# Feed-forward second product by seven Strassen block products, with GpSimd adding the blocks of h

## Chip, core and metric

One core of a Trainium2 chip runs the whole program. The metric is device microseconds of one execution; lower is better.

## What is computed

One layer of a diffusion transformer: sequence mixers, then a feed-forward block on 1024 tokens of width 1024, hidden width 2816, all in float32. The change touches the feed-forward block and the layer norm that ends the kernel:

```python
def conv_ffn(h, w_up, conv_w, conv_b, w_down, grid_rows):
    a, g = jnp.split(h @ w_up, 2, axis=-1)                 # first product
    ...
    a = dwconv3x3(a.reshape(...), conv_w).reshape(bsz, t, f) + conv_b
    return (jax.nn.gelu(a, approximate=False) * g) @ w_down  # second product
...
x_new = layer_norm(ALPHA * x_new + mx[5] * ffn_x, ln2_g[l], ln2_b[l])
```

## The kernel before

Every large product is made in three TensorE passes of 128x512: each operand is split into a high part (a copy by ScalarE rounded to float32r) and a low part (the remainder, by VectorE or GpSimd), and `mm3` adds high by high, high by low and low by high in PSUM.

**First product, `ffn_up`.** It runs over 22 hidden tiles ("units", f = 0 to 21) of 128 columns, each for the a half and the g half. It is already done by Strassen's method: per unit seven block products in the order k = 1, 2, 6, 5, 7, 3, 4, each of 12 matmuls. `prepare` makes the weight blocks five products ahead: the sums of blocks and the low parts on GpSimd (`pool.tensor_tensor`, 11 of them in a unit), the high parts on ScalarE. `Unit.after(k)` hangs the other work behind the products: behind k = 3 the convolution of the unit (eight VectorE operations), behind k = 6 of the next unit its GELU (ScalarE), behind k = 5 of the next unit the product with the gate (`Unit.finish`, VectorE), which stores the tile h of 128x1024 to DRAM (`hd[f]`). The buffers of this stage come from one ring of 13 (`S`), in order of allocation. In this stage the order on every engine is the order of the code (`pinned`).

**Second product, `ffn_down`.** Two passes, g = 0 and 1, over the tokens in halves of 512. In each pass all 22 hidden tiles are multiplied into eight PSUM banks (four token tiles t by two column halves c): 22 x 4 x 2 x 3 = 528 matmuls, 1056 in both. `down_load` loads weights `in_w_down` (tile `r`) and h (tile `hr`) on SyncE's queue and splits them into `dwh`, `dwl` and `dh`; the scheduler orders this stage. `down_first` prepares the first three hidden tiles beside the last unit of `ffn_up`, and their 72 matmuls open the stage. The last 3 tiles of pass 0 and the last 7 of pass 1 are held back (`late`) and multiplied token tile by token tile, so that VectorE can finish one token tile (`gate` product, `residual`, statistics, `finish`: the layer norm `ln_g`, `ln_b`, and the store of `out`) while TensorE works on the next.

## Time and profile before

| | |
|---|---|
| three runs | 1334.07, 1337.91, 1340.23 us; median 1337.91 |
| profiled execution | 1334.04 us; span of its instructions 1332.1 us |
| TensorE matmul, VectorE, ScalarE, GpSimd busy | 1275.0 (96%), 963.9 (72%), 536.7 (40%), 307.0 us (23%) |
| granted TensorE clock, mean | 0.995 |
| 700 to 1060 us (first product): TensorE, VectorE, GpSimd | 354.79, 264.25, 269.82 of 360 us; DMA 105 GB/s |
| 1078 to 1206 us (second product, most of pass 0): TensorE, VectorE, GpSimd | 124.71, 66.51, 4.34 of 128 us; DMA 180 GB/s |
| 1206 to 1332 us (most of pass 1): TensorE, VectorE, GpSimd | 116.46, 79.22, 0.00 of 126 us; DMA 154 GB/s |

Times in the trace count from the start of the span. PE is TensorE, DVE VectorE, ACT ScalarE, POOL GpSimd, SPq SyncE's queue, which issues nearly all DMAs. An instruction's row gives its start, its length, its engine, output and inputs, and in brackets how long the engine was idle before it and what ended that. A PE row's length holds the pipeline; the pace of matmuls is read from the starts of consecutive rows. The record lacks a few matmuls.

### The profile page before, as it was taken

How to read it: one execution, taken by the hardware profiler on the slowest of the kernel's cores; microseconds unless marked ns; L12 is line 12 of the kernel's file. 1: busy time of each engine (PE TensorE's matmuls, PEld its weight loads, DVE VectorE, ACT ScalarE, POOL GpSimd, SP SyncE). 2: the span in 40 equal slices, each digit the busy share in tenths (PEclk: the TensorE clock that was granted, in tenths of full speed). 3: DMA queues.
4: the chain of work that ended last, by engine and by line, in shares of the span. 5: the costliest groups of instructions: out<-in, count | busy, mean ns of one | idle time of the engine just before them, and what ended most of it. 6: DMA issues, size and time to landing. Idle time of an engine off the chain costs nothing. (4 is left out here: it accounts for less than half of the span.)

```text
span 1332.1 us, 17666 instructions
## 1 busy us (share of the span) xinstructions
PE 1275.0 (96%) x6480; PEld 1069.2 (80%) x6480; DVE 963.9 (72%) x1744; ACT 536.7 (40%) x972; POOL 307.0 (23%) x249
## 2 busy tenths in 40 slices
PE   4999999999999999999988999999999999999997
PEld 3888888899888887777876888888888878888885
DVE  7868975686769679689787787776667754359447
ACT  4835444433342241444553444444444434324420
POOL 0000000000000000000026777787767730000000
PEclk9999999999999999999998999999999999999999
DMA  9763343114122155355382344222222319448522
GB/s 332 257 199 118 108 131 126 48 62 143 35 87 88 48 163 190 100 199 191 127 238 81 125 158 158 104 102 95 96 68 76 119 65 322 142 136 273 175 94 81
DMA packets 88103, 181.82 MB, mean 136 GB/s; under 512 B 8768, under 2 KB 29904, under 8 KB 88016
## 3 DMA queue, kind: packets, MB, share of 16 engines
q1 hardware_dynamic: 85424, 171.25, 38.5%
q0 software_dynamic: 2592, 9.44, 1.9%
q8 instruction: 51, 0.84, 0.3%
q14 instruction: 36, 0.29, 0.1%
HBM read 150.23 MB, written 30.43 MB: 136 GB/s over the span
## 5 line engine op out<-in xcount | busy, mean ns | idle before, releaser
L57 DVE SCALAR_TENSOR_TENSOR psA<-a,par,psA 128x945 f32<-128x945 f32 (+2 forms) x176 | 215.9, 1227 | 21.7 <-ACT psA L57 16.2
L57 PE MATMUL psA<-x,wf 128*128 128x512 f32 x708 | 173.6, 395 | 6.5 <-ACT h L57 3.4
L57 PE MATMUL psB<-xk,wf 128*128 128x512 f32 x672 | 176.8, 390 | 1.0 <-ACT s L57 1.0
L57 PEld LDWEIGHTS psA<-x,wf 128*128 128x128 f32 x708 | 134.6, 190 | 36.2 <-ACT psA L57 4.3
L57 PEld LDWEIGHTS psB<-xk,wf 128*128 128x128 f32 x672 | 126.2, 188 | 27.9 <-ACT s L57 1.4
L57 POOL TENSOR_TENSOR wf<-raw,wf 128x512 fp32r<-128x512 f32 x95 | 122.4, 1297 | 54.4 <-ACT wf L57 54.3
L57 PE MATMUL psA<-xh,wh 128*128 128x512 f32 x320 | 126.7, 396 | 2.0 <-ACT wh L57 1.2
L57 PE MATMUL psA<-xh,wl 128*128 128x512 f32 x320 | 126.1, 394 | 0.1
L57 PE MATMUL psA<-xl,wh 128*128 128x512 f32 x320 | 125.9, 393 | 0.0
L57 POOL DMA_DIRECT2D wd<-pk x16 | 8.7, 543 | 498.9 <-ACT pk L57 461.3
L57 DVE TENSOR_TENSOR dwl<-r,dwh 128x512 fp32r<-128x512 f32 x74 | 48.4, 689 | 81.0 <-ACT dwh L57 80.9
L57 PE MATMUL psB<-x,wf 128*128 128x512 f32 x384 | 104.7, 389 | 0.0
L57 PE MATMUL psB<-dwh,dh 128*128 128x512 f32 x296 | 97.2, 389 | 2.6 <-ACT dh L57 2.6
L57 PE MATMUL psA<-dwh,dh 128*128 128x512 f32 x296 | 97.3, 390 | 0.5 <-DVE fy L57 0.5
L57 PEld LDWEIGHTS psB<-x,wf 128*128 128x128 f32 x384 | 72.1, 188 | 15.4 <-issue 0.2
L57 ACT CAST dwh<-r 128x512 fp32r<-128x512 f32 x74 | 43.0, 620 | 102.8 <-PE psA L57 63.4
L57 ACT CAST wh<-r 128x512 fp32r<-128x512 f32 x76 | 44.5, 619 | 84.3 <-PE psA L57 55.9
L57 ACT CAST wf<-raw 128x512 fp32r<-128x512 f32 x95 | 58.7, 618 | 47.8 <-PE psA L57 27.4
L57 DVE TENSOR_TENSOR a<-psA,s 128x512 f32<-128x512 f32 x39 | 27.0, 691 | 61.9 <-PE psA L57 61.9
L57 PEld LDWEIGHTS psA<-xh,wh 128*128 128x128 f32 x320 | 60.2, 188 | 14.0 <-ACT wh L57 1.6
L57 PEld LDWEIGHTS psA<-xh,wl 128*128 128x128 f32 x320 | 60.2, 188 | 12.3 <-DVE wl L57 0.5
L57 PEld LDWEIGHTS psA<-xl,wh 128*128 128x128 f32 x320 | 60.2, 188 | 11.8 <-issue 0.2
(324 smaller groups left out, 2761.2 us busy)
## 6 DMA issues: line engine op xcount, KB each, us to landing
r<-in_w_down SPq DMA_DIRECT2D x82, 256.0 KB, 3.2
raw<-in_wup SPq DMA_DIRECT2D x38, 512.0 KB, 4.9
ada<-in_ada SPq DMA_DIRECT2D x32, 512.0 KB, 4.4
r<-in_win SPq DMA_DIRECT2D x56, 256.0 KB, 2.9
hr<-hd SPq DMA_DIRECT2D x41, 256.0 KB, 4.3
hd<-h SPq DMA_DIRECT2D x20, 512.0 KB, 3.0
adat<-in_ada SPq DMA_DIRECT2D x16, 512.0 KB, 6.5
wd<-pk POOLq DMA_DIRECT2D x16, 512.0 KB, 3.6
```

Of the source, the lines that this page charges most:

```text
L57: ins = f(*args, **kw)
```

## The change

The second product is done by seven block products too. Tokens, hidden tiles and output columns are halved: h in blocks of 512 tokens by 11 hidden tiles, weights in blocks of 11 hidden tiles by 512 columns. A step is one product k and one of its 11 hidden tiles f: 4 token tiles by 3 passes, 12 matmuls. There are 77 steps, i = 0 to 76, in the order k = 1, 2, 6, 5, 3, 7, 4; 924 matmuls. Products 1, 6, 7 and 4 add up in four banks X, products 2, then 5 and 3, in four banks Y.

- **Sums of h.** For units f < 11, `sums` subtracts the two token halves of h on GpSimd and stores the 128x512 result (`s3`). For f of 11 and more, `fetch` loads the tile of unit f - 11 back and GpSimd makes two more sums (`s12`), one behind product 1 and one behind product 2 of the next unit; they go to DRAM too. That makes 11 + 22 GpSimd operations. In `ffn_up` the order on TensorE, VectorE and ScalarE is unchanged.
- **Sums of weights.** They are made on VectorE in the second product (`sum_t`, `sum_t4`, `sum_t3`: 22 + 11 + 11 operations), in tiles `tk`, `tv`, `tr` that stay in SBUF; before product 3, 11 more subtractions are made on h.
- **Operands.** `load` issues a step's DMAs eight steps ahead, `high` splits five steps ahead on ScalarE, `low` four steps ahead on VectorE (GpSimd for steps 3 and 4); eight pairs of split tiles are in flight. Every piece is 128x512 (256 KB). Three steps are prepared by `down_first`, 36 matmuls in place of 72. The SyncE queue is in program order; its load into `tv` (made by `stores`), the first of step 8, waits for TensorE's last use of step 2 (`dwv`), whose memory it takes.
- **Ends.** The four quarters of the output come ready at different times: work on them is put into a list `todo`, from which one piece a step is taken on VectorE (two in the first five steps of product 7). Products 5 and 7 hold their last 3 steps back and product 4 its last 5, to be multiplied by token tiles in the order (2, 3), (0), (1). Rows of x (`fx`) come by GpSimd's queue, a half tile each, and the first 512 tokens are stored by it too.

On GpSimd in the first product, one unit of the second half. Before (`wf` is a low part, `raw` a weight block, `s` its sum):

```order
L57 TENSOR_TENSOR wf_8410<-raw_8216,wf_8410 128x512
L57 TENSOR_TENSOR wf_8437<-s_8435,wf_8437 128x512
L57 TENSOR_TENSOR raw_8217<-raw_8216,raw_8217 128x512
L57 TENSOR_TENSOR wf_8453<-s_8433,wf_8453 128x512
L57 TENSOR_TENSOR raw_8216<-raw_8216,s_8435 128x512
L57 TENSOR_TENSOR wf_8479<-raw_8217,wf_8479 128x512
L57 TENSOR_TENSOR wf_8495<-raw_8216,wf_8495 128x512
L57 TENSOR_TENSOR wf_8517<-raw_8217,wf_8517 128x512
```

After; `s_8596` is the new tile of sums, `h_8509` the tile loaded back:

```order
L57 TENSOR_TENSOR wf_8489<-raw_8285,wf_8489 128x512
L57 TENSOR_TENSOR wf_8518<-s_8516,wf_8518 128x512
L57 TENSOR_TENSOR raw_8286<-raw_8285,raw_8286 128x512
L57 TENSOR_TENSOR wf_8534<-s_8514,wf_8534 128x512
L57 TENSOR_TENSOR raw_8285<-raw_8285,s_8516 128x512
L57 TENSOR_TENSOR wf_8560<-raw_8286,wf_8560 128x512
L57 TENSOR_TENSOR s_8596<-h_8509,h_8487 128x512
L57 TENSOR_TENSOR wf_8576<-raw_8285,wf_8576 128x512
L57 TENSOR_TENSOR s_8596<-s_8596,h_8509 128x512
L57 TENSOR_TENSOR wf_8600<-raw_8286,wf_8600 128x512
```

Two operations more stand between the low parts, the first of them behind a load.

On VectorE, second product. Before, in pass 1, only splitting while TensorE multiplies:

```order
L57 TENSOR_TENSOR dwl_10623<-r_10625,dwh_10622 128x512
L57 TENSOR_TENSOR dwl_10623<-r_10629,dwh_10622 128x512
L57 TENSOR_TENSOR dh_10624<-hr_10633,dh_10624 128x512
L57 TENSOR_TENSOR dhw_10780<-hr_10789,dhw_10780 128x512
L57 TENSOR_TENSOR dwl_10662<-r_10664,dwh_10661 128x512
L57 TENSOR_TENSOR dwl_10662<-r_10668,dwh_10661 128x512
L57 TENSOR_TENSOR dh_10663<-hr_10672,dh_10663 128x512
```

After, from the first use of product 3's finished banks, in product 7 (`fl` is a step's low part, `fy` an output half tile, `fx` its row of x, `bnd` its statistics):

```order
L57 TENSOR_TENSOR fy_9632<-fy_9632,psB_9617 128x512
L57 TENSOR_TENSOR fy_9656<-fy_9656,psB_9618 128x512
L57 TENSOR_TENSOR fl_10671<-dr_10608,fh_10670 128x512
L57 TENSOR_TENSOR fl_10671<-tk_9317,fh_10670 128x512
L57 TENSOR_TENSOR fy_9681<-fy_9681,psA_9619 128x512
L57 TENSOR_TENSOR fy_9704<-fy_9704,psA_9619 128x512
L57 TENSOR_TENSOR fl_10693<-dr_10628,fh_10692 128x512
L57 TENSOR_TENSOR fl_10693<-tk_9317,fh_10692 128x512
L57 TENSOR_TENSOR fy_9632<-fy_9632,gate_9322 128x512
L57 SCALAR_TENSOR_TENSOR fy_9632<-fx_10732,fy_9632 128x512
L57 BN_STATS bnd_9633<-fy_9632 128x6
L57 TENSOR_TENSOR fy_9656<-fy_9656,gate_9322 128x512
```

Between two steps' low parts there now stands the finishing of the first 512 tokens' second halves.

On VectorE at the end. Before, the last token tile, from its second half's product with the gate:

```order
L57 TENSOR_TENSOR fy_11045<-psB_10153,gate_9962 128x512
L57 SCALAR_TENSOR_TENSOR fy_11045<-fx_11046,fy_11045 128x512
L57 BN_STATS bnst_11048<-fy_11045 128x6
L57 BN_AGGR mvt_11097<-bnst_11048 128x2
L57 TENSOR_SCALAR vet_11099<-mvt_11097 128x1
L57 SCALAR_TENSOR_TENSOR fy_11045<-fy_11045,mvt_11097,ln_g 128x512
L57 RECIPROCAL rst_11100<-nwt_11102 128x1
L57 SCALAR_TENSOR_TENSOR fy_11045<-fy_11045,mvt_11097,ln_g 128x512
L57 TENSOR_TENSOR nwt_11102<-vet_11099,rst_11100 128x1
L57 SCALAR_TENSOR_TENSOR nwt_11102<-nwt_11102,rst_11100 128x1
L57 SCALAR_TENSOR_TENSOR rst_11100<-nwt_11102,rst_11100 128x1
L57 SCALAR_TENSOR_TENSOR fy_11045<-fy_11045,rst_11100,ln_b 128x512 x2
```

After, the last four rows of token tile 7 and the start of token tile 4; token tile 5 follows in the same way:

```order
L57 SCALAR_TENSOR_TENSOR fy_10406<-fy_10406,finmv_11130,ln_g 128x512
L57 SCALAR_TENSOR_TENSOR fy_10406<-fy_10406,finrs_11132,ln_b 128x512
L57 SCALAR_TENSOR_TENSOR fy_10406<-fy_10406,finmv_11130,ln_g 128x512
L57 SCALAR_TENSOR_TENSOR fy_10406<-fy_10406,finrs_11132,ln_b 128x512
L57 TENSOR_TENSOR fy_10418<-psB_9314,gate_9322 128x512
L57 SCALAR_TENSOR_TENSOR fy_10418<-fx_11169,fy_10418 128x512
L57 BN_STATS bnd_10419<-fy_10418 128x6
L57 BN_AGGR finmv_11174<-bnd_10419 128x2
L57 TENSOR_SCALAR finve_11175<-finmv_11174 128x1
L57 RECIPROCAL finrs_11176<-finw_11177 128x1
L57 TENSOR_TENSOR finw_11177<-finve_11175,finrs_11176 128x1
L57 SCALAR_TENSOR_TENSOR finw_11177<-finw_11177,finrs_11176 128x1
```

The product with the gate of token tile 4, whose bank is the last but one, stands behind eight layer norm operations of tiles 6 and 7.

The diff, cut to its core:

```diff
@@ Unit.after (first product, after each product k) @@
+            if k in (1, 2) and b.made:
+                b.made.sums()[k - 1]()
...
-                    b.prev = None
+                    b.prev.fetch()
+                    b.made = b.prev
...
+                if f == FT - 1:
+                    for part in b.made.sums():
+                        part()
                 self.conv()
@@ Unit, new @@
+        def fetch(self):
+            if self.f >= FT // 2:
+                self.h1 = self.new((2, 512), nm="h1")
+                self.b.nc.sync.dma_start(self.h1.rearrange("p g t -> p (g t)"), self.b.hd[self.f - FT // 2])
+        def sums(self):
+            b, pool, f = self.b, self.b.nc.gpsimd, self.f
+            def one():
+                if f < FT // 2:
+                    s3 = b.S((2, 512), nm="s3")[:, 0]
+                    pool.tensor_tensor(out=s3, in0=self.h[:, 0], in1=self.h[:, 1], op=ALU.subtract)
+                    b.nc.sync.dma_start(b.s3[f], s3)
+                else:
+                    self.s12 = self.new((2, 512), nm="s12")
+                    pool.tensor_tensor(out=self.s12[:, 0], in0=self.h1[:, 1], in1=self.h[:, 1], op=ALU.add)
+            def two():
+                if f >= FT // 2:
+                    s = self.s12
+                    pool.tensor_tensor(out=s[:, 1], in0=s[:, 0], in1=self.h1[:, 0], op=ALU.subtract)
+                    (b.nc.sync if f < FT - 2 else b.nc.gpsimd).dma_start(b.s12[f - FT // 2], s)
+            return one, two
+    HF = FT // 2
@@ down_first (prepared beside the last unit) @@
+            nc.sync.dma_start(r[f][:, 0], self.h_part(0, 0, f))
+            nc.sync.dma_start(r[f][:, 1], self.w_part(0, 0, f))
...
@@ ffn_down, new (the old one, down_load, load_xnew and finish go) @@
+        order = (1, 2, 6, 5, 3, 7, 4)
+        plan = [(k, f) for k in order for f in range(HF)]
+        N, LD, LP = len(plan), 8, 4
+        first = {k: HF * i for i, k in enumerate(order)}
+        group = {5: 3, 7: 3, 4: 5}
+        X = [self.bank("B"), self.bank("B"), *(lambda p: (p[:, 0], p[:, 1]))(self.pair())]
+        kq = [self.kp.tile([P, 8, 512], F32, tag="kq", bufs=2, name=self.name("tk")) for _ in range(2)]
...
+        def load(i):
+            k, f = plan[i]
+            if k == 1 and f == 8:
+                stores()
+            if k == 1:
+                nc.sync.dma_start(t1[f], self.w_part(0, 0, f))
+                if i < 3:
+                    return
+            r = raws[i] = raw()
+            h = {1: (0, 0), 2: (0, 1), 3: (0, 1), 4: (1, 1)}.get(k)
+            src = self.h_part(*h, f) if h else self.s3[f][:, :] if k == 7 else self.s12[f][:, 1 if k == 6 else 0]
+            nc.sync.dma_start(r[:, 0], src)
+            w = {2: (1, 0), 3: (1, 1)}.get(k)
+            if w:
+                nc.sync.dma_start(r[:, 1], self.w_part(*w, f))
+            if k == 3:
+                exs[i] = self.Rt(nm="s2")
+                nc.sync.dma_start(exs[i], self.s12[f][:, 1])
+        def load_t(f):
+            e = ts[f] = extra()
+            for phi in range(2):
+                nc.sync.dma_start(e[:, phi], self.w_part(phi, 1, f))
+        def sum_t(f):
+            e = ts.pop(f)
+            tt(out=t1[f], in0=e[:, 0], in1=t1[f], op=ALU.subtract)
+            tt(out=t2[f], in0=e[:, 1], in1=t1[f], op=ALU.subtract)
...
+        def high(i):
+            k, f = plan[i]
+            if i % 8 < 3:
+                x = forms[i] = [self.Wt((2, 512), nm="dw") for _ in range(2)]
+            else:
+                x = forms[i] = [dn.tile([P, 2, 512], F32R, tag=t, bufs=5, name=self.name(t)) for t in ("fh", "fl")]
+            if k == 3:
+                tt(out=raws[i][:, 0], in0=raws[i][:, 0], in1=exs.pop(i), op=ALU.subtract)
+            if k in (2, 3):
+                nc.scalar.copy(x[0], raws[i])
+            else:
+                for j, src in enumerate(source(i)):
+                    nc.scalar.copy(x[0][:, j], src)
+        def low(i):
+            k, f = plan[i]
+            x = forms[i]
+            on = nc.gpsimd if i < 5 else nc.vector
+            if k in (2, 3):
+                on.tensor_tensor(out=x[1], in0=raws[i], in1=x[0].bitcast(F32), op=ALU.subtract)
+            else:
+                for j, src in enumerate(source(i)):
+                    on.tensor_tensor(out=x[1][:, j], in0=src, in1=x[0][:, j].bitcast(F32), op=ALU.subtract)
+            raws.pop(i)
+        def multiply(i, t):
...
+            b = (Y if k in (2, 5, 3) else X)[t]
+            mm(b, hi[:, 0, s], hi[:, 1], start=k in (1, 2, 5) and f == 0, stop=False, skip_group_check=True)
+            mm(b, lo[:, 0, s], hi[:, 1], start=False, stop=False, skip_group_check=True)
+            mm(b, hi[:, 0, s], lo[:, 1], start=False, stop=f == HF - 1, skip_group_check=True)
...
+        def out(t, c, bank, add):
+            x, y = {}, new_y(t)[:, half[c]]
+            def fetch():
+                x[0] = dn.tile([P, 512], F32, tag="fx", bufs=3, name=self.name("fx"))
+                nc.gpsimd.dma_start(x[0], self.xnew[t][:, half[c]])
+            def begin():
+                if add:
+                    tt(out=y, in0=y, in1=bank, op=ALU.add)
                 else:
+                    fetch()
+                    tt(out=y, in0=bank, in1=gate[:, half[c]], op=ALU.mult)
+            def mid():
+                fetch()
+                tt(out=y, in0=y, in1=gate[:, half[c]], op=ALU.mult)
+            def end():
+                self.residual(x[0], y, st[t][:, c, :])
+            if add:
+                return begin, mid, end
+            return begin, end
...
+        def chain(*ts):
+            n = len(ts)
+            mv, ve, rs, w = (x[:, 0:n] for x in smalls())
+            for j, t in enumerate(ts):
+                nc.vector.bn_aggr(out=mv[:, j, :], in_=st[t])
+                stat[t] = mv[:, j, 0:1], rs[:, j:j + 1]
+            nc.vector.tensor_scalar(out=ve, in0=mv[:, :, 1], scalar1=EPS, scalar2=None, op0=ALU.add)
+            self.rsqrt2(rs, ve, n, w)
+        def last(t, c):
+            m, r = stat[t]
+            y, s = ys[t][:, half[c]], half[c]
+            nc.vector.scalar_tensor_tensor(out=y, in0=y, scalar=m, in1=lng[:, s], op0=ALU.subtract, op1=ALU.mult)
+            nc.vector.scalar_tensor_tensor(out=y, in0=y, scalar=r, in1=lnb[:, s], op0=ALU.mult, op1=ALU.add)
+            (nc.gpsimd if t < 4 else nc.sync).dma_start(self.out[t * P:(t + 1) * P, s], y)
...
+        sums = [(load_t, sum_t, 6, 2), (load_t4, sum_t4, first[6] + 1, 1), (load_t, sum_t3, first[5] - 2, 2)]
+        for i in range(N):
+            k, f = plan[i]
+            if i + LD < N:
+                load(i + LD)
+            for l, _, at, by in sums:
+                j = i - at + 3
+                if j >= 0 and j % by == 0 and j // by < HF:
+                    l(j // by)
+            if i + LP + 1 < N:
+                high(i + LP + 1)
+            if i + LP < N:
+                low(i + LP)
+            if i == 0:
+                u = self.prev
+                u.new = lambda shape, nm: extra()
+                u.gelu()
+                u.fetch()
+                u.finish()
+                for part in u.sums():
+                    part()
+            for _, g, at, by in sums:
+                j = i - at
+                if j >= 0 and j % by == 0 and j // by < HF:
+                    g(j // by)
...
+            n = group.get(k, 0)
+            if f < HF - n:
                 for t in range(4):
+                    multiply(i, t)
+            elif f == HF - 1:
+                if k == 4:
+                    for g in todo:
+                        g()
+                    todo = []
+                for part in ((2, 3), (0,), (1,)):
+                    for t in part:
+                        for j in range(i - n + 1, i + 1):
+                            multiply(j, t)
+                    for t in part:
+                        if k == 5:
+                            nc.scalar.copy(new_y(4 + t)[:, half[1]], Y[t])
+                        elif k == 7:
+                            b, *e = out(4 + t, 1, X[t], True)
+                            b()
+                            todo += e
+                        else:
+                            for g in out(4 + t, 0, X[t], False):
+                                g()
+                    if k == 4:
+                        chain(*(4 + t for t in part))
+                        for t in part:
+                            for c in range(2):
+                                last(4 + t, c)
...
+            if f == 0 and k == 5:
+                for x in zip(mids, ends):
+                    todo += x
+            if f == 0 and k in (6, 7):
+                o = [out(t, 0 if k == 6 else 1, Y[t], True) for t in range(4)]
+                todo += [x[0] for x in o]
+                mids, ends = [x[1] for x in o], [x[2] for x in o]
+                if k == 7:
+                    fin = [lambda t=t, c=c: last(t, c) for t in range(4) for c in range(2)]
+                    todo += [mids[0], both(ends[0], mids[1]), both(ends[1], mids[2]), both(ends[2], mids[3]), both(ends[3]),
+                             both(lambda: chain(0, 1, 2, 3), fin[0]), *fin[1:]]
+            for _ in range(2 if k == 7 and f < 5 else 1):
+                if todo:
+                    todo.pop(0)()
```

More of the change, by code (lines that the diff above doesn't have):

```diff
@@ L243, in build @@
             self.hd = [self.dp.tile([P, T], F32, name=f"hd{f}") for f in range(FT)]
+            self.s12 = [self.dp.tile([P, 2, 512], F32, name=f"s12_{f}") for f in range(FT // 2)]
+            self.s3 = [self.dp.tile([P, 512], F32, name=f"s3_{f}") for f in range(FT // 2)]
             self.xr = [self.dp.tile([P, 2, 512], F32, name=f"xr{j}") for j in range(4)]
@@ L1218, in ffn_up @@
         go(u1, 7)
[L1219 removed]
+        tt(out=u1.r[1], in0=u1.x, in1=u1.r[0], op=ALU.add)
         self.prepare(self.at + 5)
@@ L1255, in ffn_up @@
         self.prepare(self.at + 5)
-        u1.finish((u1.x, u1.r[:, 1]))
+        u1.finish((u1.x, u1.r[1]))
         u2.conv()
-        self.prev = u2
+        u1.sums()[0]()
+        self.prev, self.made = u2, None
         for f in range(3, FT):
@@ new lines, in high, with low @@
+        def high(dst, f):
+            nc.scalar.copy(dst, r[f])
+        def low(dst, hi, f):
+            nc.gpsimd.tensor_tensor(out=dst, in0=r[f], in1=hi.bitcast(F32), op=ALU.subtract)
+        def ahead(k):
+            y = self.ready
+            if k in (2, 7):
+                f = (2, 7).index(k)
+                y[f] = [self.Wt((2, 512), nm="dwh")]
+                high(y[f][0], f)
+            elif k in (6, 3):
+                f = (6, 3).index(k)
+                y[f].append(self.Wt((2, 512), nm="dwl"))
+                low(y[f][1], y[f][0], f)
+            elif k == 5:
+                v = self.kp.tile([P, 4, 512], F32R, tag="vt", bufs=1, name=self.name("dwv"))
+                y[2] = [v[:, 0:2], v[:, 2:4]]
+                high(y[2][0], 2)
+                low(y[2][1], y[2][0], 2)
@@ L1447, in ffn_down @@
                     self.row(n, r)
-            gate, lng, lnb = rows
-            ys = []
-            for t in range(4):
-                y = dn.tile([P, D], F32, tag="fy", bufs=4, name=self.name("fy"))
-                if g == 1:
-                    x = self.load_xnew(dn, 4 + t)
-                    st = self.small([2, 6], nm="bnst")
-                for c in range(2):
-                    for l in late:
-                        work(t, c, *l)
-                    s = slice(c * 512, (c + 1) * 512)
-                    nc.vector.tensor_tensor(out=y[:, s], in0=banks[t][c], in1=gate[:, s], op=ALU.mult)
-                    if g == 1:
-                        self.residual(x, y, s, st[:, c, :])
-                if g == 1:
-                    self.finish(y, 4 + t, lng, lnb, st)
-                ys.append(y)
@@ L1495, in load_xnew @@
[L1495 to L1514 removed]
+                gate, lng, lnb = rows
@@ L1517, in layout, with residual @@
+        assert not todo
+    def residual(self, x, y, st):
+        nc = self.nc
+        nc.vector.scalar_tensor_tensor(out=y, in0=x, scalar=ALPHA, in1=y, op0=ALU.mult, op1=ALU.add)
+        nc.vector.bn_stats(out=st, in_=y)
 def layout(x):
```

221 lines of the change are left out of this document (92 added, 129 removed).

## Prediction

> **What bounds the kernel now.** I read the page first, then who waited for whom on TensorE in the second product, the start and end of that stage in order of time, VectorE's pace there, and last GpSimd and the DMA by stretches.
>
> ```profile
> core 0 of [0], span 1332.1 us
> PE 1275.0 (96%) x6480; PEld 1069.2 (80%) x6480; DVE 963.9 (72%) x1744; ACT 536.7 (40%) x972; POOL 307.0 (23%) x249
> PE psB L57 <- ACT dh L57: 2.6, 1, 2.6
> PE psB L57 <- POOL dwl L57: 0.7, 1, 0.7
> PE psA L57 <- DVE fy L57: 0.5, 1, 0.5
> 1075.45 2.88 PE L57 MATMUL psB<-xk,wf 128*128 128x512 f32 x12
> 1078.17 0.39 PE L57 MATMUL psB<-dwh,dhw 128*128 128x512 f32 x1
> 1304.85 18.15 PE psB L57 x80
> 1323.00 0.02 issue
> ```
>
> TensorE is the bound: 96% busy, and in the whole second product (from 1078) it waited three times, 3.8 us together. Twelve matmuls take 1078.17 - 1075.45 = 2.72 us, 0.2267 each. The second product opens at 1078.17, and by the chain of work that ended last its matmuls end at 1323.0: 244.8 us, of which 1056 x 0.2267 = 239.4 are pace, 3.8 waits and 1.6 unexplained. What follows 1323.0 is VectorE and a store:
>
> ```profile
> 1323.02 0.69 DVE L57 TENSOR_TENSOR fy<-psB,gate 128x512 f32<-128x512 f32 x1 [1.59 <-PE psB L57]
> 1323.75 0.69 DVE L57 SCALAR_TENSOR_TENSOR fy<-fx,fy 128x512 f32<-128x512 f32 x1
> 1324.48 0.69 DVE L57 BATCH_NORM_STATS2 bnst<-fy 128x6 f32<-128x512 f32 x1
> 1325.21 0.21 DVE L57 BATCH_NORM_AGGREGATE mvt<-bnst 128x2 f32<-128x12 f32 x1
> ...
> 1327.29 0.16 DVE L57 SCALAR_TENSOR_TENSOR rst<-nwt,rst 128x1 f32<-128x1 f32 x1
> 1327.48 1.41 DVE L57 SCALAR_TENSOR_TENSOR fy<-fy,rst,ln_b 128x512 f32<-128x512 f32 x2
> 1202.70 1.29 DVE L57 TENSOR_TENSOR dwl<-r,dwh 128x512 fp32r<-128x512 f32 x2
> 1203.91 0.69 DVE L57 TENSOR_TENSOR dh<-hr,dh 128x512 fp32r<-128x512 f32 x1
> 1204.52 1.29 DVE L57 TENSOR_TENSOR dwl<-r,dwh 128x512 fp32r<-128x512 f32 x2
> ```
>
> VectorE ends at 1327.48 + 1.41 = 1328.9 and the span at 1332.1 (first row above): the tail behind the last matmul is 9.1 us, 3.2 of it the store. VectorE's own pace is to be read here too: independent operations follow each other every 0.60 us (1202.70, two later 1203.91, the next 1204.52), dependent ones every 0.73 (1323.02, 1323.75, 1324.48, 1325.21).
>
> **The matmuls.** 1056 become 924: 132 x 0.2267 = -29.9 us, all on the path, since TensorE is the bound there. The three waits go with the code that made them: -3.8.
>
> **GpSimd in the first product.** One TensorE unit is 84 x 0.2267 = 19.04 us.
>
> ```profile
> L57 POOL TENSOR_TENSOR wf<-raw,wf 128x512 fp32r<-128x512 f32 x78 | 100.2, 1293 | 43.2 <-ACT wf L57 43.1
> L57 POOL TENSOR_TENSOR raw<-raw,raw 128x512 f32<-128x512 f32 x16 | 27.6, 1724 | 0.0
> 1000.00:1040.00 40.00, 40.00 (x178) 33.14 (x177) 27.23 (x28) 17.96 (x28) 29.86 (x25) 1.00 0.19 69
> 787.60 1.81 DVE L57 CUSTOM_DVE_ANT_0 ada<-ada,silc,par 128x1024 f32<-128x1024 f32 x1
> 788.30 2.27 POOL L57 TENSOR_TENSOR raw<-raw,raw 128x512 f32<-128x512 f32 x1
> 790.53 1.29 POOL L57 TENSOR_TENSOR wf<-s,wf 128x512 fp32r<-128x512 f32 x1
> 785.49 0.68 DVE L57 TENSOR_TENSOR h<-h,r 128x512 f32<-128x512 f32 x1
> raw<-in_wup SPq DMA_DIRECT2D x38, 512.0 KB, 4.9
> ```
>
> In the stretch from 1000 us GpSimd is busy 29.86 of 40 (the fifth pair of columns). A unit has 11 operations of 1.29: 14.2. Units from 11 on get two more, 16.8 of 19.04; the earlier ones one, 15.5. The low parts are begun four to five products before use, at least 10.9 us, so a low part that comes 2.6 later still comes in time: 0. What hides it is that lead; were it gone, the cost would be up to 2.6 x 11 = 29. The first sum waits for a tile of 512 KB loaded back, issued behind product 5, three products and more (8 us) ahead; loads of that size into `raw` land in 4.9. No wait is removed here, so no gain either.
>
> By the Trainium skill, "SBUF — State Buffer", section "Who interferes with whom", a VectorE operation with two SBUF inputs and a GpSimd operation that reads SBUF lock each other out. The rows agree: next to the 1.81 us operation on `ada` and `silc` GpSimd takes 2.27, else 1.29. By that rule units from 12 on, where VectorE has only the 0.68 us product `h<-h,r` of this kind, would lose up to about a microsecond each, 17.8 of 19.04, and the sum would be the same.
>
> **The start of the stage.** 36 matmuls are ready in place of 72, 8.2 us of cover for what step 3 needs.
>
> ```profile
> 1077.26 10.06 DVE L57 SCALAR_TENSOR_TENSOR psA<-a,par,psA 128x945 f32<-128x945 f32 x8 [0.85 <-ACT psA L57]
> 1078.15 2.37 POOL L57 TENSOR_TENSOR dwl<-dr,dwh 128x1024 fp32r<-128x1024 f32 x1
> 1057.82 36.60 SPq L57 DMA_DIRECT2D r<-in_w_down  x3
> 1094.47 0.42 SPq L57 DMA_DIRECT2D hr<-hd  x1
> r<-in_w_down SPq DMA_DIRECT2D x80, 256.0 KB, 3.2
> L57 ACT CAST dwh<-r 128x512 fp32r<-128x512 f32 x74 | 43.0, 620 | 102.8 <-PE psA L57 63.4 <-PE psB L57 20.3 <-DMA r<-in_w_down 14.4
> 1110.00:1114.00 4.00, 4.00 (x19) 3.31 (x18) 1.90 (x3) 1.72 (x3) 0.00 (x0) 1.00 1.03 355
> 1211.00:1217.00 6.00, 6.00 (x28) 4.96 (x27) 5.86 (x13) 3.33 (x6) 0.00 (x0) 1.00 0.86 249
> 1217.00:1223.00 6.00, 6.00 (x28) 4.98 (x27) 6.00 (x16) 1.87 (x4) 0.00 (x0) 1.00 0.96 307
> ```
>
> Before, SyncE's queue stood from 1057.82 to 1094 and TensorE still lost only 2.6. Now it can start when product 7 of the last unit frees `tk`, 5.4 us ahead of the stage. Up to step 3 it carries three pieces, three rows of 512 KB and two pieces, 2.9 MB: 8.2 us at 355 GB/s, and about 2 to land, so +5 in the stage. Two casts of 0.6 and two GpSimd operations of 1.29 make +8.8, against 8.2. Bounds: 0, and 5 (the old waits of 2.6 and 0.7 and half as much again); I take +1.5, nearest to the arithmetic. The queue's wait for `tv` holds all loads from step 8 on until step 2 is multiplied, +8.2; step 8 is needed at +21.8, so 0. VectorE's convolution ends at +9.2, and step 5, its first, is due at +13.6: 0.
>
> **DMA.** `load` and the sums of weights fetch 34, 26, 25 and 45 pieces in steps 3-13, 14-24, 25-35 and 36-46: 130 x 0.262 MB, with four pieces of x 35.1 MB in 44 x 2.72 = 119.7 us, 293 GB/s. The last stretches above carry 355, 249 and 307 GB/s at a DMA share of 1.03, 0.86 and 0.96, so 290 to 345 when full. The top stretch (11.8 MB in 29.9 us) falls behind by some 6 us, and pieces are issued eight steps, 21.8 us, ahead. Hidden: 0. Its ends: nothing at 293 and more, +10 at 270 (35.1 MB / 0.27 = 130 us).
>
> **VectorE up to product 7.**
>
> ```profile
> L57 DVE TENSOR_TENSOR kq<-kq,F 128x1024 f32<-128x1024 f32 x56 | 67.5, 1216 | 0.2
> ```
>
> Steps 0 to 54: convolution and gates 11.3, 64 low parts x 0.60, 22 of double width x 1.22, 44 sums of weights and 11 of h x 0.60, four adds, four finishing triples x 2.0: 120 us in 55 x 2.72 = 149.6. It keeps up: 0.
>
> **VectorE from product 7 to the end.** The order lists 138 operations from the first use of the finished Y banks:
> - 34 low parts x 0.60 = 20.4
> - 8 adds from a bank x 0.60 = 4.8
> - 12 triples (gate, residual, statistics), 0.73 + 0.73 + 0.60, some interleaved: 12 x 2.0 = 24.0
> - 16 half tiles of layer norm, two operations, 1.41 by the row of 1327.48: 22.6
> - 4 chains of small operations. 1325.21 to 1327.48 is 2.27 with two operations of 0.66 inside; bounds 0.95 and 2.27, I take 1.7, since ScalarE's root lies within: 6.8
>
> That is 78.6, and 1 for x behind the stores on GpSimd's queue: 79.6. TensorE's 22 steps are 59.8. So here VectorE is the bound: it ends 79.6 after the begin of product 7, plus 3.2 for the store, 82.8, where TensorE and the old tail would give 59.8 + 9.1 = 68.9. Cost +13.9. When TensorE waits for a bank that VectorE hasn't read yet, that is within this chain and isn't counted again. Bounds: 110 wide operations at 0.60 and 28 small ones at 0.16 are 70.5, +4.8; all wide ones at 0.73 are 91.6, about +26.
>
> **Sum.** -29.9 - 3.8 + 1.5 + 13.9 = -18.3: the profiled execution's 1334.04 becomes 1315.7. That execution is the fastest of before, 3.9 under the median of 1337.91, which would give 1319.6; I take 1317 for a median.
>
> **Rivals.**
> - DMA is the bound in steps 3 to 46. For it: 293 GB/s asked, and one full stretch that did 290. Against: 345 and 320 in the others. At 270 it gives 1317 + 10 = 1327; to cancel all gain it would have to fall to 250. The Trainium skill, "DMA: Bandwidth & Descriptors", section "Measured", says to batch to 1 MiB for 75% of peak; pieces of 256 KB would fall short of 290 by its table. The stretches were made of such pieces and reached 307 and 355, so the trace speaks against it.
> - All finishing stays hidden as far as VectorE's bound allows (70.5 us): 1317 - 9 = 1308. For it: operations of different tiles alternate. Against: inside a triple and a half tile each waits for the one before.
> - GpSimd becomes the bound in units 11 to 21, and the kernel slower. At 1.72 an operation (the row above, beside a VectorE operation of two SBUF inputs) 13 are 22.4, 3.3 over a unit: 11 units lose 36, less some 8 of lead: 1317 + 28 = 1345. It decides from 1.65 us an operation. Against: at 1000 us, with conv and gates running, GpSimd took 1.29.
>
> **How the numbers follow.** VectorE's end chain 0.60, DMA bound 0.22, finishing hidden 0.10, GpSimd bound 0.05, anything else 0.03. Half a per cent, 6.7 us, is what a measurement of this kernel can tell from nothing: faster is below 1331.2. The first and third case are all below it, the second mostly (0.15 of 0.22): 0.85 faster, 0.09 the same, 0.06 slower. The range reaches from the case of hidden finishing, 1307, over that of the DMA to 1330.
>
> **What would show it.** Of the profile after: PE 2.72 a step with a wait of 1 to 2 us at step 3; GpSimd 16.8 us a unit and no wait of PE for `wf`; VectorE without a pause from product 7 on and its work some 16 us past the last matmul, waits of PE for `psB` or `psA` on VectorE at the begin of product 4; the DMA share near 0.9 with no wait of PE for `fh`, `fl` or `dw` before product 7. Wrong would be: waits for low parts behind a DMA in steps 36 to 54, or for `wf` in the first product, or a tail below 12 us.

## The result, and the profile after

The changed kernel takes 1320.66 us in the median of four runs (1317.66, 1318.38, 1322.94, 1323.20), before 1335.99: a ratio of 0.9882 with a 95% interval of 0.9842 to 0.9922. The forecast was 1317.0 for a median and 1315.7 on the scale of the profiled execution, which took 1317.66. One of the nine runs of the kernel "low parts by GpSimd" in the table below took 3580.91 us; it is in that kernel's median and in none of the ratios.

The page of after, its waits of TensorE in the second product, the first matmul of that stage, and VectorE's rows at its end:

```profile
span 1315.9 us, 17639 instructions
PE 1244.5 (95%) x6348; PEld 1044.4 (79%) x6348; DVE 1016.8 (77%) x1790; ACT 550.5 (42%) x980; POOL 363.7 (28%) x309
PE psB L57 <- DVE fy L57: 2.9, 1, 2.9
PE psB L57 <- ACT fh L57: 1.5, 1, 1.5
PE psB L57 <- POOL fl L57: 1.1, 2, 0.7
PE psB L57 <- POOL dwl L57: 0.6, 1, 0.6
1076.23 0.39 PE L57 MATMUL psB<-dwh 128*128 128x512 f32 x1
1294.80 0.39 PE L57 MATMUL psA<-fl,fh 128*128 128x512 f32 x1
1230.21 1.37 DVE L57 TENSOR_TENSOR fy<-fy,psB 128x512 f32<-128x512 f32 x2 [4.13 <-PE psB L57]
1274.48 0.69 DVE L57 SCALAR_TENSOR_TENSOR fy<-fx,fy 128x512 f32<-128x512 f32 x1 [1.93 <-DMA fx<-xnew]
1288.42 0.69 DVE L57 TENSOR_TENSOR fy<-psA,gate 128x512 f32<-128x512 f32 x1 [1.81 <-PE psA L57]
1311.94 0.75 DVE L57 SCALAR_TENSOR_TENSOR fy<-fy,finrs,ln_b 128x512 f32<-128x512 f32 x1
```

From the first matmul of the second product to the end of the span ("the stage" below) it is 1315.9 - 1076.23 = 239.7 us, where it was 1332.1 - 1078.17 = 253.9: 14.3 less. The other 1.9 lie before the stage, whose start scatters from 1075.3 to 1079.9 in the runs below that leave the first product alone (once 1084.1); they aren't the change's. TensorE now ends 20.7 us ahead of the span, before 9.1, and VectorE works from 1230.21 to 1312.7 with 3.7 us of waiting inside: 1.93 for a row of x and 1.81 for token tile 2 from TensorE.

The stretches of GpSimd in the first product, and of the DMA in steps 3 to 46 (columns as before: GpSimd's busy time is the fifth pair; then granted clock, DMA share, GB/s):

```profile
980.00:1020.00 40.00, 40.00 (x178) 33.13 (x177) 27.93 (x28) 17.81 (x29) 34.72 (x28) 1.00 0.41 149
1085.00:1117.00 32.00, 29.40 (x120) 23.42 (x119) 21.13 (x26) 15.73 (x23) 11.15 (x11) 0.95 0.96 346
1117.00:1146.00 29.00, 29.00 (x129) 24.02 (x128) 26.72 (x38) 17.36 (x28) 0.00 (x0) 1.00 0.85 307
1146.00:1176.00 30.00, 30.00 (x134) 24.82 (x133) 27.07 (x45) 15.16 (x29) 0.55 (x1) 1.00 0.87 296
1176.00:1206.00 30.00, 30.00 (x133) 24.48 (x132) 23.78 (x35) 10.82 (x14) 1.64 (x3) 1.00 1.03 375
```

GpSimd is busy 34.72 of 40, 16.5 a unit, and TensorE 40.00 of 40. The DMA engines are busy for 0.85 to 1.03 of the time from 1085 to 1206, and no wait of TensorE for a load stands in the list above between step 3 and product 4.

The start of the stage, in rows of SyncE's queue, ScalarE and TensorE, and three stretches of 1 us:

```profile
1074.99 0.43 SPq L57 DMA_DIRECT2D dr<-hd  x1
1085.75 0.62 ACT L57 CAST fh<-dr 128x512 fp32r<-128x512 f32 x1 [10.46 <-DMA dr<-hd]
1086.94 0.50 PE L57 MATMUL psB<-fh 128*128 128x512 f32 x1 [1.54 <-ACT fh L57]
1089.01 0.50 PE L57 MATMUL psB<-fl,fh 128*128 128x512 f32 x1 [0.73 <-POOL fl L57]
1085.00:1086.00 1.00, 0.40 (x2) 0.00 (x0) 0.39 (x1) 0.25 (x1) 0.00 (x0) 1.00 1.06 406
1090.00:1091.00 1.00, 1.00 (x4) 0.76 (x3) 0.50 (x1) 1.00 (x3) 1.00 (x2) 0.50 1.06 408
1093.00:1094.00 1.00, 1.00 (x6) 0.83 (x5) 1.00 (x3) 0.60 (x2) 0.30 (x2) 1.00 1.02 375
```

h of step 3 was issued at 1074.99 and used at 1085.75, 10.7 us later, in which the DMA moved 358 GB/s. Behind the waits the granted clock was 0.50 until 1093: four matmuls a microsecond there. That loss stands in no wait; it is in "rest" in the table below.

### The profile page after: what moved, and what is told of

The parts are those of the page before. It is cut to its first block, busy times and chain, and to the rows that moved or that the text cites. A ratio compares the mean times of both kernels' runs of the same rounds, so it can differ in the third digit from the quotient of the medians.

```text
span 1315.9 us, 17639 instructions
## 1 busy us (share of the span) xinstructions
PE 1244.5 (95%) x6348; PEld 1044.4 (79%) x6348; DVE 1016.8 (77%) x1790; ACT 550.5 (42%) x980; POOL 363.7 (28%) x309
## 5 line engine op out<-in xcount | busy, mean ns | idle before, releaser
L57 POOL TENSOR_TENSOR wf<-raw,wf 128x512 fp32r<-128x512 f32 x95 | 123.2, 1301 | 19.9 <-ACT wf L57 19.3
L57 PEld LDWEIGHTS psA<-xh,wh 128*128 128x128 f32 x320 | 60.2, 188 | 14.3 <-ACT wh L57 1.6
L57 ACT CAST fh<-dr 128x512 fp32r<-128x512 f32 (+1 forms) x47 | 36.1, 768 | 82.1 <-PE psA L57 18.6
L57 PEld LDWEIGHTS psA<-xl,wh 128*128 128x128 f32 x320 | 60.2, 188 | 11.7 <-issue 0.2
L57 DVE TENSOR_TENSOR wl<-r,wh 128x512 fp32r<-128x512 f32 x76 | 50.1, 687 | 23.2 <-PE psB L57 13.2
L57 DVE TENSOR_TENSOR kq<-kq,F 128x1024 f32<-128x1024 f32 x56 | 67.6, 1217 | 0.2
L57 PE MATMUL psB<-kq,A 128*128 128x128 f32 x448 | 60.3, 288 | 0.8 <-ACT A L57 0.7
```

What stands on the lines that cost most here:

```text
L57: ins = f(*args, **kw)
```

## The experiments

All kernels in one table. Each ratio is to runs of before that were taken along with that kernel, so ratios are compared, not medians; stage, waits, rest and tail are those of one profile each. "Waits" are TensorE's in the stage; "rest" is what is left of the time to TensorE's end when these and 924 x 0.2267 = 209.5 us are taken off (before: 239.4); "tail" is from TensorE's end to the span's.

| kernel | median | ratio to before (95%) | stage | waits | rest | tail |
|---|---|---|---|---|---|---|
| before | | | 253.9 | 3.8 | 1.6 | 9.1 |
| after | 1320.66 | 0.9882 (0.9842 to 0.9922) | 239.7 | 6.1 | 3.4 | 20.7 |
| after, second time | 1318.32 | 0.9893 (0.9866 to 0.9919) | 242.6 | 6.3 | 6.0 | 20.8 |
| rows loaded late | 1317.59 | 0.9868 (0.9844 to 0.9892) | 236.5 | 3.6 | 2.7 | 20.7 |
| low parts by GpSimd | 1326.23 | 0.9937 (0.9911 to 0.9963) | 248.1 | 10.6 | 7.3 | 20.7 |
| eight steps held | 1322.40 | 0.9906 (0.9880 to 0.9932) | 239.6 | 9.7 | 8.7 | 11.7 |
| both of these | 1327.66 | 0.9945 (0.9925 to 0.9965) | 247.0 | 16.1 | 9.8 | 11.7 |
| sums three times | 1349.64 | 1.0115 (1.0091 to 1.0140) | 249.0 | 14.7 | 4.1 | 20.7 |
| low parts left out | 1313.37 | 0.9853 (0.9827 to 0.9878) | 235.1 | 2.9 | 1.9 | 20.7 |
| left out, eight held | 1315.97 | 0.9865 (0.9843 to 0.9887) | 235.9 | 7.9 | 6.9 | 11.7 |
| early finishing | 1310.44 | 0.9830 (0.9808 to 0.9851) | 232.0 | 2.0 | 1.2 | 19.3 |
| early, seven held | 1309.60 | 0.9821 (0.9800 to 0.9841) | 231.5 | 2.6 | 2.8 | 16.6 |
| more DMA (rows late) | 1332.28 | 0.9988 (0.9974 to 1.0001) | 254.9 | 14.1 | 10.6 | 20.7 |
| GpSimd, wait filled | 1323.97 | 0.9924 (0.9901 to 0.9947) | 245.0 | 3.9 | 4.0 | 20.7 |

**The control.** The changed kernel once more:

> The changed kernel once more, unaltered, as the measure for the others on the same chip: ratio to before 0.988, the stage (first matmul of the second product to the end of the span) 239 to 241 us, if its one profile is typical; a difference of more than 1.5 us would mean that differences of that size between the other profiles say nothing.

Measured: 242.6, so differences of up to 3 us between single profiles can be chance; what follows goes by waits and rows, and by stage only where more than that lies between. Where the 2.9 us are can be read, since 2.6 of them lie in "rest": at the start the clock stays halved for about 3 us longer, and TensorE's wait at product 4 is as long as in the first profile, but here the clock halves behind it. TensorE's row there, and three stretches of the second profile:

```profile
1268.42 0.77 PE L57 MATMUL psB<-dw 128*128 128x512 f32 x1 [2.85 <-DVE fy L57]
1094.13:1098.13 4.00, 4.00 (x13) 3.15 (x12) 4.00 (x6) 2.54 (x6) 2.70 (x3) 0.62 0.98 354
1266.00:1268.00 2.00, 0.00 (x0) 0.00 (x0) 2.00 (x4) 2.00 (x5) 0.11 (x1) 0.97 0.57 173
1268.00:1270.00 2.00, 1.58 (x4) 1.32 (x5) 1.97 (x4) 0.56 (x2) 0.00 (x0) 0.50 0.23 89
```

The times of the ten runs of this kernel go with their mean clock: 1315.33 to 1318.38 at 0.990 and 0.991, 1319.46 to 1323.20 at 0.988 to 0.986, 1326.88 at 0.984.

**The start: rows loaded late.**

```diff
-            if i == 2:
-                rows = [...]          # gate5, ln2_g, ln2_b: three loads of 512 KB
+            if i == 22:
+                rows = [...]
```

> Only the loads of the rows gate, ln_g and ln_b (three of 512 KB) are moved, from between step 2 and step 3 on SyncE's queue to step 22. After the change the second product takes 239.7 us from its first matmul (1076.23) to the end of the span (1315.9); its 36 ready matmuls run out and TensorE loses 2.6 us in three waits at step 3, and its next matmuls come at 0.32 to 0.43 us each for some 4 us. Theory 1, the DMA queue: h of step 3 is issued at 1075.0 and lands 10.7 us later, behind 1.5 MB of rows; at 390 GB/s these are 3.9 us. Without them the piece lands near 1082, the waits go, and since everything behind hangs on TensorE, the stage is 3 to 5 us shorter: 235 to 237. Theory 2, all loads in flight share the rate and the pieces of later steps move up: h of step 3 lands at most 1 us earlier and the stage stays within 1 us of 239.7. Theory 3, the stall goes but the rows collide with the loads of steps 20 to 30: a new wait of TensorE for fh or fl in steps 22 to 35, stage 237 to 240.

Measured: 236.5, where the first theory has it. The row that takes h of step 3, and the waits that are left:

```profile
1079.36 0.62 ACT L57 CAST fh<-dr 128x512 fp32r<-128x512 f32 x1 [2.98 <-DMA dr<-hd]
PE psB L57 <- DVE fy L57: 2.8, 1, 2.8
PE psB L57 <- POOL dwl L57: 0.6, 1, 0.6
PE psB L57 <- ACT fy L57: 0.2, 1, 0.2
```

The stage starts at 1077.32 here, so h of step 3 is there 2.0 us into it, in place of 9.5. The second theory, 1 us at most, is refuted by this; it is also more than the 3.9 us by which the rows alone would have held it up, because loads issued behind it share the rate: up to 1085.75 the changed kernel had moved 4.8 MB (323 GB/s from 1070.98 on), of which only 3.4 were issued ahead of that load or with it. The waits at step 3 are gone, 2.6 us, and with them the half clock behind them; no other took their place, except 0.2 at a bank. But "rest" falls by 0.7 only, since here the clock halves behind the wait at product 4. The gain of 3.2 us in the stage is no more than the scatter, and the ratios don't separate the two kernels; it is the row and the waits that show the effect. The tail is the same to 0.02: what TensorE gains at the start, the end keeps.

**The end, first pair.** GpSimd makes part of the low parts; product 4 holds eight steps; both.

```diff
                 for j, src in enumerate(source(i)):
+                    if k in (7, 4) and j:
+                        on = nc.gpsimd
...
-        group = {5: 3, 7: 3, 4: 5}
+        group = {5: 3, 7: 3, 4: 8}
-                for part in ((2, 3), (0,), (1,)):
+                for part in ((2,), (3,), (0,), (1,)) if k == 4 else ((2, 3), (0,), (1,)):
```

> The low parts of the weights in products 7 and 4 (22 operations, one of the two a step) are made by GpSimd in place of VectorE. From the begin of product 7 on VectorE has 17 operations of 0.60 fewer, 10.2 us. Theory A, the sum of VectorE's work sets the end (as the prediction had it): the stage, 239.7 us from the first matmul to the end of the span, becomes 230 to 232. Theory B, the order of the end sets it: from the last matmul on token tiles 2 and 3 (VectorE's wait for TensorE ends at 1288.4) VectorE has 24.3 us of finishing that can't begin earlier. Then only TensorE's wait of 2.85 us for VectorE at product 4 goes, and the stage becomes 236.9 (236.3 to 237.5), with the work behind the last matmul as long as before. Theory C, VectorE and GpSimd lock each other out: GpSimd's operations take 1.7 us or more in place of 1.29, VectorE's neighbours get longer too, and less than 2 us is gained or something lost.

> Product 4 holds back its last 8 steps in place of 5, and multiplies them one token tile at a time in the order 2, 3, 0, 1, so that VectorE may begin to finish token tile 2 earlier: 3 steps of 2.72 and 8 x 0.68 = 5.4 us behind the begin of product 4, near 1278.6, in place of 1288.4. Theory A (VectorE's sum of work sets the end): VectorE has the same work, the stage stays at 239.7 within 1.5. Theory B (the order of the end alone sets it): four token tiles of 6.4 us from 1278.6 end at 1304.2, 8.5 us earlier, stage 231. Theory A and B in series: VectorE is busy with low parts and the triples of product 7's quarter until 1286.6 whatever TensorE does, so four tiles of 6.4 end at 1312.2: the stage stays at 239 to 241.

> Both: GpSimd makes the low parts of the weights in products 7 and 4, and product 4 holds back 8 steps, one token tile at a time. Theory A (VectorE's sum): as with GpSimd's low parts alone, stage 230 to 232. Theory B (order alone): -11.4, 228, and the holding alone would give 231. Both in series: the one alone gives 2.9 us, the other alone none, and together they give more than the sum of the two, 6 to 11 us, stage 229 to 234; TensorE may lose a few us waiting for low parts of the last held steps, which it now needs earlier.

Measured: 248.1, 239.6, 247.0. GpSimd's help cost some 5 to 8 us: the third theory, but with the loss on VectorE's side. VectorE's groups from 1229 on in after (two rows), from 1236 on with GpSimd's help (two), and one pair of neighbours there:

```profile
L57 DVE SCALAR_TENSOR_TENSOR fy<-fy,finmv,ln_g 128x512 f32<-128x512 f32 x16 | 11.9, 746 | 0.0
L57 DVE TENSOR_TENSOR fy<-fy,gate 128x512 f32<-128x512 f32 x8 | 5.4, 680 | 0.0
L57 DVE SCALAR_TENSOR_TENSOR fy<-fy,finmv,ln_g 128x512 f32<-128x512 f32 x16 | 20.8, 1298 | 0.0
L57 DVE TENSOR_TENSOR fy<-fy,gate 128x512 f32<-128x512 f32 x8 | 11.9, 1482 | 0.0
1251.94 2.23 DVE L57 SCALAR_TENSOR_TENSOR fy<-fy,finmv,ln_g 128x512 f32<-128x512 f32 x1
1252.31 1.30 POOL L57 TENSOR_TENSOR dw<-tv,dw 128x512 fp32r<-128x512 f32 x1
```

These 24 VectorE operations took 8.9 + 6.5 = 15.4 us longer, more than the 10.2 that were taken off, so VectorE read its last X bank still later and TensorE's wait at product 4 grew from 2.9 to 6.9. Nothing else made VectorE late: ahead of the finishing behind token tile 2 it waited 1.4 us for TensorE, and for no row of x. An operation of two SBUF inputs that meets one of GpSimd's takes 2.23 in place of 0.75, while GpSimd's takes 1.30; of GpSimd's low parts behind the begin of product 7 only two took longer, 1.60 and 1.73. The Trainium skill, "SBUF — State Buffer", section "Who interferes with whom", has this as an exclusive lock between the two; these rows agree, and here it is VectorE that pays, though its row begins 0.37 us earlier. Because of this the pair doesn't decide between the theories; that eight held steps alone gain nothing (239.6) says only that VectorE isn't free earlier.

**The end, second pair.** The same relief without GpSimd:

```diff
+                    if k in (7, 4) and j:
+                        nc.scalar.copy(x[1][:, j], src)
+                        continue
```

> The low parts of the weights in products 7 and 4 are left out: ScalarE, which has time there, copies the block itself into their place, so the output differs. VectorE is relieved of the same 17 operations of 0.60 behind the begin of product 7 as when GpSimd made them, but without GpSimd beside it, which had made VectorE's operations longer (248.1 us for the stage). Theory A, the sum of VectorE's work alone sets the end: stage 239.7 - 10.2 = 229 to 231. Theory A and B in series: only TensorE's wait of 2.9 us at product 4 goes, since behind the last matmul of token tiles 2 and 3 the same 24.3 us of finishing follow: 236 to 237.5. If the stage stays near 248, it wasn't GpSimd that made the earlier kernel slow.

> The same low parts left out, and product 4 holds back 8 steps, one token tile at a time, which alone gained nothing (239.6). Theory A: as without the holding, 229 to 231. Both in series: relief and earlier token tiles together give more than the 2.9 of the one and the 0 of the other, 4 to 9 us: 231 to 236.

Measured: 235.1 and 235.9. With 10.2 us off VectorE the stage loses 4.6. Of these 0.3 are shorter waits at the start and 1.5 the clock (rest 1.9 in place of 3.4); the 2.8 that are left are TensorE's wait at product 4, as the theory in series has it. The sum of VectorE's work alone, 229 to 231, is refuted: 5.6 of the 10.2 us are missing, more than the scatter. TensorE's waits in the first of these, where none at product 4 is left, and VectorE's row where token tile 2 comes; then three rows of the second:

```profile
PE psB L57 <- ACT fh L57: 1.2, 1, 1.2
PE psB L57 <- POOL fl L57: 1.1, 2, 0.7
PE psB L57 <- POOL dwl L57: 0.6, 1, 0.6
1283.11 0.69 DVE L57 TENSOR_TENSOR fy<-psA,gate 128x512 f32<-128x512 f32 x1 [4.64 <-PE psA L57]
...
1263.71 0.69 DVE L57 TENSOR_TENSOR fy<-fy,psB 128x512 f32<-128x512 f32 x1 [1.35 <-PE psB L57]
1272.83 0.69 DVE L57 SCALAR_TENSOR_TENSOR fy<-fx,fy 128x512 f32<-128x512 f32 x1 [3.13 <-DMA fx<-xnew]
1291.38 0.69 DVE L57 TENSOR_TENSOR fy<-psA,gate 128x512 f32<-128x512 f32 x1 [2.43 <-PE psA L57]
```

Of the relief, 7.1 us turned into idling: VectorE waits 10.8 us behind its first use of the Y banks in place of 3.7, 4.64 of them ahead of token tile 2 (1.81 before), and behind that the same 24 us of finishing follow. With eight held the tail is short, 11.7, but VectorE's queue stands elsewhere, for TensorE (1.35, 2.43) and for a row of x (3.13), and TensorE's waits are 7.9. The two bounds in series are shown. That loosening both gives more than the sum is not: 235.9 lies inside the 231 to 236 expected, but relief alone gave 235.1, so the holding added nothing.

**GpSimd in the first product.** Each sum three times in units 11 to 21 (`for _ in range(3)` ahead of the two operations of `s12`).

> In units 11 to 21 GpSimd makes each sum of h three times (the same result written again): 17 operations of 1.29 us a unit, 21.9 us, in place of 13 (16.8), where TensorE's unit is 19.04. The prediction's reason why the sums cost nothing is that GpSimd has 2.2 us a unit left and the low parts are begun 11 us or more ahead. If so, the cover is now gone: 2.9 us over in each of 11 units are 32, less the lead of 11 to 13: the first product becomes 15 to 22 us longer, with waits of TensorE for wf, and nothing else changes. If the sums were hidden for another reason (GpSimd catches up in gaps that the page doesn't show, or the low parts aren't needed in time), the time stays within 4 us of the change's.

Measured: 1349.64, about 30 us longer. The first product grew by about 21 (the stage starts at 1098.7, else mostly at 1075.3 to 1079.9), with GpSimd and TensorE in one stretch, and two waits:

```profile
980.00:1020.00 40.00, 35.89 (x154) 29.08 (x153) 24.56 (x24) 14.67 (x25) 39.29 (x32) 0.98 0.37 131
PE psB L57 <- ACT s L57: 14.3, 7, 2.8
PE psB L57 <- POOL dwl L57: 11.8, 1, 11.8
```

GpSimd is busy 39.29 of 40 and TensorE 35.89. So the cover was GpSimd's spare time. The expectation missed two things. TensorE's waits in the first product aren't for `wf` but for ScalarE's copies of a bank into `s`, 14.3 us, which stand on its queue behind casts of `wf` that wait for GpSimd's sums. And the sums of the last unit stand ahead of `dwl` on GpSimd's queue, so that step 1 of the second product waited 11.8 us for it.

**The DMA.** In steps 8 to 46 a piece more each, from DRAM to DRAM.

```diff
+            if 8 <= i < 47:
+                nc.sync.dma_start(self.spare[i], self.w_part(0, 0, f))
```

> Rows loaded late (stage 236.5 us by itself), and in each step from 8 to 46 one more piece of 256 KB is copied from DRAM to DRAM on SyncE's queue, whose result nobody reads: 39 pieces, 10.2 MB, besides some 40 MB moved from 1085 to 1206. The prediction took 290 to 345 GB/s for full; the changed kernel's profile has stretches at 384 to 400 GB/s. Theory 1, full is about 400: 50 MB take 125.6 us where TensorE's 44 steps take 119.7; less what eight steps of lead absorb, the stage becomes 236 to 243. Theory 2, full is 345 or less: 145 us and more, the stage 250 to 262, with TensorE waiting for fh, fl and dw all through steps 15 to 54. If so, DMA is the next bound of this change, otherwise it had room for a quarter more.

Measured: 254.9, 18.4 above the same kernel without the pieces. Two stretches of this run, and the chain at the end of product 5, whose banks ScalarE must copy out before product 3 adds to them:

```profile
1117.00:1146.00 29.00, 29.00 (x129) 23.73 (x128) 23.07 (x31) 15.47 (x23) 0.00 (x0) 1.00 1.04 391
1176.00:1206.00 30.00, 25.69 (x99) 19.06 (x98) 25.75 (x40) 12.76 (x21) 2.19 (x4) 0.94 1.03 382
1206.89 1.04 ACT L57 CAST fh<-dr 128x1024 fp32r<-128x1024 f32 x1 [2.52 <-DVE dr L57]
1210.70 1.07 ACT L57 COPY fy<-psA 128x512 f32<-128x512 f32 x2
1212.30 0.80 PE L57 MATMUL psB<-fh 128*128 128x512 f32 x1 [7.33 <-ACT fy L57]
```

Full is 380 to 390 GB/s in these stretches, more than the prediction's 290 to 345, and still a quarter more is too much. The time is in the range of the second theory, but its premise, 345 GB/s or less, doesn't hold, and 7.9 of the 18.4 us lie in "rest", which no theory had. Most of the waiting isn't where it had been put either: 3.3 us are for `fl` and `dw`, but ScalarE's casts come late, the copies of a bank stand behind them on its queue, and TensorE waits 7.3 for the bank.

**Two versions meant to be faster.** The rows loaded late; for the quarters that are finished in products 7 and 4, the gate and x are applied to the part already copied out while VectorE has time, and ScalarE copies the bank.

```diff
+                def left():                       # in products 5 and 3, behind y *= gate
+                    self.scale(x[0], y)           # y = ALPHA * x + y
+                def bring():
+                    nc.scalar.copy(v[0], bank)
+                def gated():
+                    tt(out=v[0], in0=v[0], in1=gate[:, half[c]], op=ALU.mult)
+                def join():
+                    tt(out=y, in0=y, in1=v[0], op=ALU.add)
+                    nc.vector.bn_stats(out=st[t][:, c, :], in_=y)
-                for part in ((2, 3), (0,), (1,)):
+                for part in ((2, 3), (0, 1)) if k == 4 else ((2, 3), (0,), (1,)):
```

The second holds seven steps and makes their low parts first (`4: 7`, and no piece of the list in product 4 behind its first step).

> A version meant to be faster, nothing left out. Rows loaded late (236.5 us for the stage by itself). For the second and third quarter of the output the product of the part that ScalarE has copied out with the gate, and the addition of x, are made in products 5 and 3, so that behind product 7's begin a half tile takes VectorE three operations in place of four (8 fewer); the bank is copied out by ScalarE, so TensorE needn't wait for VectorE at product 4; one piece a step, and token tiles 0 and 1 finished together. By the sum of VectorE's work: 8 x 0.6 = 4.8 and 1.5 for the pair: 230. By the order of the end: 2.8 for the wait and 1.5 for the pair: 232. I expect 230 to 233. Wrong if VectorE has no room for the 16 operations in products 5 and 3: then TensorE waits for fl there and the stage is 236 or more.

> A version meant to be faster: the one with the early finishing (stage 232.0), and product 4 holds back 7 steps in place of 5; behind its first step VectorE makes the low parts before the pieces that finish product 7's quarter. In the former VectorE stood idle for 4.6 us before token tile 2 came from TensorE; with 7 steps held, tiles 2 and 3 are ready 2.7 us earlier, and the pieces fill the gap. By the order of the end the stage becomes 228 to 230. It stays at 232 or grows if the low parts of the held steps come too late and TensorE waits for them (fl, dw) inside the held part.

Measured: 232.0, and 231.5, not the 228 to 230 expected. The 2 us between the two theories for the first lie within the scatter; that VectorE idles for 4.64 us ahead of token tile 2 speaks for the order of the end. The rows of token tile 2 in the first and in the second:

```profile
1282.64 0.69 DVE L57 TENSOR_TENSOR fy<-psA,gate 128x512 f32<-128x512 f32 x1 [4.64 <-PE psA L57]
1282.13 0.69 DVE L57 TENSOR_TENSOR fy<-psA,gate 128x512 f32<-128x512 f32 x1 [1.91 <-PE psA L57]
```

The gap shrank by 2.7, but token tile 2 came only 0.6 earlier in its stage: in this profile TensorE had lost 0.6 more by waits and 1.6 by the clock. Both versions beat both kernels, at 0.983 and 0.982 of before; between the two nothing is decided.

**The clock.** The kernel with GpSimd's help once more, its wait of 6.9 us filled with 30 matmuls that nobody reads:

> The kernel in which GpSimd makes low parts, and 30 matmuls of 128x512 into product 3's banks, which nobody reads any more, are put between products 7 and 4: 30 x 0.2267 = 6.8 us of work that fills TensorE's wait of 6.9 us for VectorE there. In that kernel the granted clock was 0.50 behind the wait and the first matmuls of product 4 came at 0.43 us, some 12 of them, 2.5 us lost; also in one of two profiles of the changed kernel behind its 2.8 us wait. Theory 1, the clock falls because TensorE stands idle: with the wait filled it stays at 1.00 until the end of product 4, TensorE ends 2 to 3 us earlier (225 us from the first matmul in place of 227.4), and the stage is 0 to 1.5 us shorter than 248.1, since VectorE waited 1.4 for token tile 2. Theory 2, the clock falls for another reason (load, or a time of its own): 0.5 to 0.9 shows in the stretch behind the filler as before, and TensorE's end stays at 227 or later.

Measured: TensorE ends at 224.2 in place of 227.4, the stage is 245.0. The stretches behind the wait in the kernel with GpSimd's help, unfilled, and behind the filler:

```profile
1273.00:1275.00 2.00, 2.00 (x6) 1.60 (x5) 2.00 (x3) 0.00 (x0) 1.18 (x2) 0.50 0.05 18
1264.00:1268.00 4.00, 4.00 (x19) 3.30 (x19) 3.96 (x5) 0.63 (x2) 2.31 (x4) 1.00 0.40 131
1268.00:1272.00 4.00, 3.85 (x18) 2.87 (x17) 3.96 (x7) 1.14 (x2) 1.44 (x2) 1.00 0.41 131
```

The clock stayed at 1.00 behind the filler, so there it had fallen because TensorE stood idle. One profile of each is little, but behind the other waits of over 6 us (6.92 with both of the first pair, 7.33 with more DMA, 11.76 with the sums three times) it was 0.50 as well. The stage's 3.1 us are within the scatter. The 3.2 us of TensorE's end lie in the rest (4.0, the filler's 6.8 taken off, in place of 7.3); some of them belong to the start, where the clock was low for a shorter time in this profile, and how many can't be told.

## Why the prediction was right

The time lay in the range, and the likeliest case (VectorE's end chain) is the one that came. Its steps:

- **Matmuls, -29.9, and old waits, -3.8:** as forecast; twelve matmuls still take 2.72. Of the three old waits the one for `dwl`, 0.7, didn't go; it is still there with 0.6 and is counted under the start.
- **GpSimd, 0:** right, and for the reason given: 16.5 us a unit (forecast 16.8), no wait for `wf`; at 21.9 the cover is gone.
- **Start, +1.5: too small.** Waits of 0.6, 1.5 and 1.1, and 1.8 more in "rest": 5. The failing step is "about 2 to land, so +5 in the stage": h of step 3 was there at +9.5. The prediction counted 2.9 MB up to step 3 and let them land one after the other; but 4.8 MB had moved by then, since loads issued behind it were in flight too, and with the rows moved away the waits vanished. The halved clock behind the waits wasn't in the sum at all.
- **DMA, 0:** right. The full rate of 290 to 345 GB/s was too low (375 over 30 us here), and the margin is still smaller than that suggests.
- **VectorE up to product 7, 0:** right; it stood idle for 4.13 us at 1230.
- **End, +13.9: right in size, 14.5** (tail 11.6 longer, wait of 2.9), in part by luck. VectorE's work was 78.8, forecast 78.6. But it took 82.5 for it, with 3.7 of waiting where the forecast has 1 for x and the sign "without a pause"; and it began 1.8 ahead of product 7 (1232.05 by TensorE's rows), since product 3's first bank is ready that much earlier. The two errors, 2.7 and 1.8, all but cancel. The upper bound in that paragraph, 91.6, doesn't follow from its figures: 110 x 0.73 and 28 x 0.16 are 84.8, about +19; nothing else uses it. The picture behind it was half right: "VectorE is the bound" as a sum of 138 operations would have let 10.2 us less work gain 10. It gained some 2.8, since the last 24 us can't begin before TensorE delivers token tile 2. "When TensorE waits for a bank ... that is within this chain" was right only as long as VectorE isn't relieved.

Together -29.9 - 3.8 + 5 + 14.5 = -14.2, and the stage measures -14.3. The sum has -18.3: it is 4 off in the stage, nearly all at the start. The profiled execution lost 16.4 in all; most of the other 2 us lie before the stage, where the change has no part in them. The median's forecast of 1317 was put 2.6 below what the sum gives (1319.6), with no reason given; 1320.66 was measured. The distance from the profile's 1317.66 to that median goes with the clock, 0.990 in the profiled execution and 0.987 in the two slowest.

## What to carry over

When fewer matmuls leave an engine behind as the bound of the end, count its work and also ask from which delivery its last piece can begin: the two limits act in series, and loosening one moves the idle time to the other. Price a wait of TensorE with the slow matmuls behind it, and prefer an order of loads and bank copies that has no wait over one that has a short one. Work that fitted into GpSimd's spare time was free in the first product; at the end of this kernel, beside VectorE operations that read pairs of SBUF operands, moving work to GpSimd cost VectorE more than it took off.
